# A hybrid encoder trunk: attention and recurrence issued in fixed rounds on TensorE

## The chip, the cores and the metric

The kernel runs on 1 core of one Trainium2 chip. Its time is device microseconds from launch to end, lower is better. A core has five engines with a queue each: PE (TensorE, matrix products and transposes), DVE (VectorE), ACT (ScalarE), POOL (GpSimd) and SP (SyncE, which issues most transfers). Products are written to PSUM, which has eight banks of 512 float32 columns for each of 128 partitions; DVE and ACT read them from there.

## What is computed

Two layers over 1024 tokens of width 1024. Layer 0 sends one input projection to two head groups: A, a recurrence with a delta rule (RWKV-7, 8 heads of 64), and B, sparse attention (8 heads of 64, one shared key and value, a mask that an index score chooses). The outputs are gated, joined and projected back. Layer 1 is gated linear attention. Each layer ends in a layer norm. The part that matters here, cut:

```python
# A, per token: state S of each head (64 x 64)
sa = einsum('bhvk,bhk->bhv', S, -kk_t)
S = S * w_t[:, :, None, :] + sa[..., None] * b_t[:, :, None, :] + v_t[..., None] * k_t[:, :, None, :]
y = einsum('bhvk,bhk->bhv', S, r_t)
# B, per block of 128 queries
s = einsum('bqhd,bqkd->bqhk', qb, k_sel) * (B_HEAD_DIM ** -0.5)
p = softmax(where(valid, s, -1e30))
o = einsum('bqhk,bqkd->bqhd', p, v_sel)
# both gated, joined, projected, then layer norm
y = concatenate([ya * silu(g_a), yb * silu(g_b)], -1) @ e_w_out
h = layer_norm(DN_ALPHA * h + y)
```

## The kernel before

The program is written in a tile framework: the author writes operations, and the framework allots buffers, adds semaphores and puts the instructions of each engine in an order by a simulated timeline. An engine then runs its queue in that order. `inorder` can pin an instruction to the order of the program text; with `PIN = 0` (line 35) it does nothing, so that the order on PE is the framework's own.

The change concerns one stage, from about 475 to 805 us of the profile. It holds three things.

**Attention.** For each of 8 tiles of 128 queries, `att_logits` forms for each head up to two banks of logits (L811, L812, into banks "s"); DVE adds the mask and takes the maximum (L813); ACT takes the exponential (L822), after every second head (`HG = 2`). `att_out` transposes the weights (L849, bank "st"), and the copies to SBUF (L851) go to DVE and ACT half and half (`EVD`). The products with the values (L833) collect in bank "po"; L864 multiplies by the gate and L865 stores the tile.

**Recurrence.** The 1024 tokens are 16 chunks of 64; two chunks are a unit, so there are 8 units. `products` (L978, bank "g", four bursts for a unit, each read by ACT at L980 and by DVE at L981 and L982) and `increments` (L987, bank "x") prepare a unit. `substitute` inverts its triangular blocks: POOL takes the diagonal blocks out (`mm`, L995, through the helper line L83), DVE sums them (`md`, L997), two transfers through DRAM bring them into another layout (L998, L1001), POOL runs 15 dependent steps (L1009, L1010), two more transfers bring the result back (L1013, L1015), and POOL spreads it (`TT`, L1017, again L83). `offdiag` completes the inverse in four steps on PE (L1035, L1044, L1054, L1063), the first after a transpose on DVE (`Tn`, L1030). `chain` then carries the state through the two chunks, three dependent steps each: Z (L1080), U (L1091 and L1096), Y (L1103), with copies on DVE and ACT between them (L1082 and L1083, L1097 and L1098, L1111 and L1113). Z and U of all heads lie in bank "zu", the outputs and states in bank "sy". `finish` normalises, gates and stores a unit's output.

**Output projection.** When attention has been issued in full, `open_pieces` frees its memory and loads the projection weights: 16 loads (L155), each split by ACT (L159) and POOL (L83). `piece` is one of 16 blocks of 128 tokens by 512 columns, 24 matmuls each (L764 to L766).

**Order.** `chain` calls `slot` six times for each unit. A slot asks the attention generator for some estimated microseconds (`att`, with the credits `ATT`), issues the preparation of the unit two ahead (`PREP`), and the off-diagonal steps of the next unit (`OFF`). In `PREP` the second half of the products ("q") and the whole of `substitute` ("s") come in slot 2; the loads for the second chunk stand directly before its products. The first two units are prepared before the chain starts. Buffers: `td`, `mm`, `md` and `BK` are single, `W` has 5, `RUV` 7.

Of the kernel before, what the change touches and what calls it, by code (L numbers as in the profile page):

```python
# [21 lines left out]
P = 128  # L22
SEQ = 1024
NT = 8
# [10 lines left out]
PIN = 0  # L35
# [7 lines left out]
FIN = 2  # L43
# [8 lines left out]
ATT, ATT1, ATT2, FC = (2.2, 1.2, 1, 10)  # L52
# [11 lines left out]
def trunk(ctx: ExitStack, tc: tile.TileContext, x, positions, e_w_in, a_mu, a_w0, a_w2, a_a0, a_a2,  # L64
# [10 lines left out]
    def cut(f, out, *ins):  # L75

        n = out.shape[1]
        each = 1
        for m in out.shape[2:]:
            each *= m  # L80
        w = max(1, PIECE // each)
        for a in range(0, n, w):
            f(out[:, a:min(n, a + w)], *(z[:, a:min(n, a + w)] for z in ins))  # L83
# [4 lines left out]
    def gmul(out, a, b):  # L88
        cut(G.tensor_mul, out, a, b)
# [671 lines left out]
    def out_piece(pt, yh, yl, wb):  # L761
        for k in range(NK):
            wh, wl = wb[k]
            PE.matmul(pt, yh[:, k, :], wh, start=(k == 0), stop=False)  # L764
            PE.matmul(pt, yh[:, k, :], wl, start=False, stop=False)  # L765
            PE.matmul(pt, yl[:, k, :], wh, start=False, stop=(k == NK - 1))  # L766
# [17 lines left out]
    open_psum("ps1", 0, s=2)  # L784
# [10 lines left out]
    def inorder(ins):  # L795
        if PIN:
            tc.keep_in_program_order(ins)

    def att_logits(i, w):

        n = P * (i + 1)
        qT = aw([P, 8, P], "qT", 2, F32R)
        nc.sync.dma_start(f32(qT), d_q[i])
        bias = cmask[:, 256 - n:] if i < 2 else bias_s[:, soff[i]:soff[i] + n]
        mx, m, rsum = aw([P, 8, 2], "mx", 2), aw([P, 8], "am", 2), aw([P, 8], "rsum", 2)
        ps = [aw([P, SEQ], "p", PB) for h in range(8)]
        w.extend((ps, rsum))
        for h in range(8):
            for z, (a, b) in enumerate(banks(n)):
                pt = ptile("s")[:, :b - a]  # L810
                inorder(PE.matmul(pt, qT[:, h, :], KH2[:, a:b], start=True, stop=False))  # L811
                inorder(PE.matmul(pt, qT[:, h, :], KL[:, a:b], start=False, stop=True))  # L812
                V.tensor_tensor_reduce(ps[h][:, a:b], pt, bias[:, a:b], 1.0, -3e38, op0=ALU.add, op1=ALU.max,  # L813
                                       accum_out=mx[:, h, z:z + 1])
            yield n / 1200
            if h % HG == HG - 1:
                hs = slice(h + 1 - HG, h + 1)
                if i >= 4:
                    V.tensor_max(mx[:, hs, 0], mx[:, hs, 0], mx[:, hs, 1])
                V.tensor_scalar(m[:, hs], mx[:, hs, 0], -0.125, None, op0=ALU.mult)  # L820
                for k in range(h + 1 - HG, h + 1):
                    A.activation(ps[k][:, :n], ps[k][:, :n], AF.Exp, scale=0.125, bias=m[:, k:k + 1],  # L822
                                 accum_out=rsum[:, k:k + 1])

    def att_out(i, w):
        ps, rsum = w
        po = ptile("po")

        def values(kt, pT):
            last = None  # L830
            for c in range(0, 512, PVN):
                for s in (1, 0):
                    last = after(last, PE.matmul(po[RS[s], c:c + PVN], v_tm[:, kt, :], pT[s][:, c:c + PVN],  # L833
                                                 start=(kt == 0 and c == 0), stop=(kt == i), skip_group_check=True))


        rb = aw([P, 8, CH], "rb")
        V.tensor_scalar(rsum, rsum, 2.0, None, op0=ALU.mult)
        V.reciprocal(rsum, rsum)
        A.copy(rb, rsum[:, :, None].to_broadcast([P, 8, CH]))  # L840
        g = aw([P, 4, P], "g")
        nc.sync.dma_start(g, d_gate[4:8, :, i * P:(i + 1) * P].rearrange("j p t -> p j t"))
        last = None
        for kt in range(i + 1):
            pT = []
            for s in range(2):
                pt = ptile("st")
                for j in range(4):
                    inorder(PE.transpose(pt[:, j * P:(j + 1) * P], ps[2 * j + s][:, kt * P:(kt + 1) * P], ident))  # L849
                pT.append(aw([P, 512], "pT", 4))  # L850
                (V.tensor_copy if (s + kt) % 4 in EVD else A.copy)(pT[s], pt)  # L851
                yield 0.45
                if s == 0 and last is not None:
                    values(kt - 1, last)
                    yield 1.0
            last = pT
        pt = ptile("st")
        for j in range(4):
            inorder(PE.transpose(pt[:, j * P:(j + 1) * P], rb[:, 2 * j:2 * j + 2, :].rearrange("p s d -> p (s d)"), ident))
        g2 = g.rearrange("p j t -> p (j t)")  # L860
        V.tensor_mul(g2, pt, g2)
        yield 0.45
        values(i, last)
        V.tensor_mul(g2, po, g2)  # L864
        nc.sync.dma_start(d_y[4:8, :, i * P:(i + 1) * P].rearrange("j p t -> p j t"), g)  # L865
        yield 1.0

    def attention():

        w = []  # L870
        yield from att_logits(0, w)
        for i in range(NT):
            w, o = [], att_out(i, w)
            m = att_logits(i + 1, w) if i + 1 < NT else iter(())
            r = 8 / (3 * i + 4)
            x = 0
            for c in o:
                yield c
                x += r
                while x >= 1:  # L880
                    x -= 1
                    c = next(m, None)
                    if c is not None:
                        yield c
            yield from m
# [64 lines left out]
    def load_unit(u):  # L950

        BK, BD = rt([P, 8, P], "BK"), rt([P, 8, P], "BD")
        nc.sync.dma_start(BK.rearrange("p (j c) t -> p j c t", c=2), d_bk[:, :, 2 * u:2 * u + 2, :])
        nc.sync.dma_start(BD.rearrange("p (j c) t -> p j c t", c=2), d_bd[:, :, 2 * u:2 * u + 2, :])
        U_[u] = dict(BK=BK, BD=BD, AT=[], W=[], MAB=rt([P, 8, CH], "MAB", 2))

    def load_chunk(u, cc):
        c = 2 * u + cc
        S = ATB[c % 6]
        vs = d_vt[c * CH:(c + 1) * CH].rearrange("t (j s d) -> t s j d", s=2, d=CH)  # L960
        for s in range(2):
            G.memset(S[RS[1 - s], :, s, 0:CH], 0.0)
            nc.sync.dma_start(S[RS[s], :, s, :], d_ar[RS[s], :, c, :])
            nc.sync.dma_start(ruv(c)[RS[1 - s], :, s, :], vs[:, s])
        U_[u]["AT"].append(S)

    def products(u, cc):

        U = U_[u]
        BK, AT = U["BK"], U["AT"][cc]  # L970
        W = rt([P, 4, 4, CH], "W", 5)
        U["W"].append(W)
        MABv = U["MAB"].rearrange("p (j c) t -> p j c t", c=2)
        for s in range(2):
            b_, k2_ = RS[s], RS[1 - s]
            pt = ptile("g")
            for j in range(4):
                inorder(PE.matmul(pt[:, j * P:(j + 1) * P], BK[:, j * 2 + cc, :], AT[:, j, s, :], start=True, stop=True))  # L978
# [276 lines left out]
    for _ in ag:  # L1255
        pass
# [265 lines left out]
```

## Time and profile before

| | us |
|---|---|
| median of 3 runs | 1338.23 (1331.89 to 1341.52) |
| the profiled execution, whole | 1340.62 |
| its span in the profile | 1338.9 |
| PE busy in the span | 1225.0 |
| DVE busy | 799.2 |
| ACT busy | 584.1 |
| POOL busy | 442.8 |

The span runs from the first to the last instruction; 1.7 us of the profiled execution lie outside. The mean granted TensorE clock is 0.952 of full speed. "Busy" of PE counts the time in which some matmul is in flight. A label such as L83 or L159 is a helper's line and holds instructions of many tiles. "Idle before" is the time that the engine stood still just ahead of an instruction, and the arrow names what ended the wait.

### The profile page before, as it was taken

What the parts mean: (1) busy time and instruction counts of PE and PEld (TensorE: products, weight loads), DVE (VectorE), ACT (ScalarE), POOL (GpSimd) and SP (SyncE); (2) the same over time, 40 slices, a digit from 0 to 9 for tenths busy, and PEclk for the clock granted to TensorE, in tenths of its full rate; (3) what the DMA queues carried; (4) which work ended last, traced back from release to release, by engine and by line L of the source; (5) the groups of instructions that cost most, each with busy time, mean ns of one, the idle gap of its engine ahead of it and who ended that gap; (6) DMA issues with size and microseconds to landing.
All of it is one profiled execution on the core that took longest, in us unless ns stands there. A gap on an engine that the chain in (4) does not pass through costs nothing.

```text
span 1338.9 us, 22002 instructions
## 1 busy us (share of the span) xinstructions
PE 1225.0 (91%) x8141; PEld 959.8 (72%) x8141; DVE 799.2 (60%) x1856; ACT 584.1 (44%) x1217; POOL 442.8 (33%) x749
## 2 busy tenths in 40 slices
PE   7998798999889968889899799999999999998997
PEld 6986585666666756667667578776678878887785
DVE  5246769999999546578677545870511124453666
ACT  5247767769732335546455351132830123332100
POOL 3233731453447432444444360143030331142000
PEclk9998799898899979999899789999999999999999
DMA  6102311442515478245433287562010220023221
GB/s 204 41 1 79 111 40 32 125 111 71 150 53 144 109 205 205 61 102 146 99 79 81 75 258 251 189 203 63 1 38 25 63 63 1 1 64 123 82 91 59
DMA packets 164780, 130.51 MB, mean 97 GB/s; under 512 B 61441, under 2 KB 138289, under 8 KB 164673
## 3 DMA queue, kind: packets, MB, share of 16 engines
q1 hardware_dynamic: 161872, 122.72, 31.9%
q10 hardware_dynamic: 2800, 6.39, 1.5%
q8 instruction: 64, 1.05, 0.3%
q14 instruction: 44, 0.35, 0.1%
HBM read 86.08 MB, written 42.99 MB: 96 GB/s over the span
## 4 chain that ended last, share of the span: by engine, by line
PE 39%; DVE 20%; DMA 15%; POOL 11%; issue 10%; ACT 4%; SPq 2%; DVEq 0%; POOLq 0%; ACTq 0%
DVE junk L677 7%; PE dn L174 4%; PE dn L176 4%; PE dn L175 4%; POOL itmp L1009 2%; POOL Xt L1010 2%; PE op L766 2%; PE op L764 2%; PE op L765 2%; PE gt L197 2%; PE gt L196 2%; PE gt L198 2%; POOL wlo L83 2%; DMA wraw<-in_e_w_in_dram 2%; DMA d_t<-Xt 1%
## 5 line engine op out<-in xcount | busy, mean ns | idle before, releaser
L83 POOL TENSOR_TENSOR wlo<-wraw,whi 128x256 fp32r<-128x256 f32 (+1 forms) x160 | 116.1, 755 | 260.0 <-ACT whi L159 202.2
L174 PE MATMUL dn<-xh,chi 128*128 128x512 f32 x336 | 138.1, 411 | 3.8 <-DVE sh L503 2.6
L176 PE MATMUL dn<-xh,clo 128*128 128x512 f32 x336 | 138.2, 411 | 0.0
L175 PE MATMUL dn<-xl,chi 128*128 128x512 f32 x336 | 137.3, 409 | 0.0
L159 ACT CAST whi<-wraw 128x512 fp32r<-128x512 f32 (+1 forms) x80 | 48.8, 613 | 133.2 <-PE dn L175 67.8
L174 PEld LDWEIGHTS dn<-xh,chi 128*128 128x128 f32 x336 | 66.4, 198 | 23.9 <-issue 5.2
L176 PEld LDWEIGHTS dn<-xh,clo 128*128 128x128 f32 x336 | 66.3, 197 | 20.4 <-issue 6.5
L175 PEld LDWEIGHTS dn<-xl,chi 128*128 128x128 f32 x336 | 66.2, 197 | 17.9 <-issue 4.2
L83 POOL TENSOR_TENSOR clo<-craw,chi 128x256 fp32r<-128x256 f32 x84 | 75.5, 927 | 1.0
L411 DVE SCALAR_TENSOR_TENSOR sc<-rl,wi_s,sc 128x384 f32<-128x384 f32 (+5 forms) x42 | 45.8, 1090 | 23.1 <-ACT rl L406 20.7
L184 POOL CAST chi<-craw 128x1024 fp32r<-128x1024 f32 x21 | 24.8, 1180 | 102.2 <-PE dn L175 84.2
L83 POOL TENSOR_TENSOR vg<-vg,sg 128x256 f32<-128x256 f32 x32 | 24.1, 775 | 99.4 <-DVE vg L1444 54.5
L822 ACT ACTIVATE p<-p,am 128x128 f32<-128x128 f32 (+7 forms) x64 | 49.1, 768 | 17.9 <-DVE am L820 17.6
L849 PE MATMUL st<-ident,p 128*128 128x128 f32 x288 | 50.8, 294 | 4.5 <-ACT pT L851 4.3
L764 PE MATMUL s<-whi,yh 128*128 128x512 f32 x128 | 51.5, 405 | 2.7 <-ACT yh L1184 1.6
L813 DVE CUSTOM_DVE_ANT_0 p<-s,bias_s 128x512 f32<-128x512 f32 (+1 forms) x80 | 45.7, 588 | 13.1 <-PE s L812 11.9
L677 DVE TENSOR_SCALAR_CACHE_REDUCE junk<-khi,Hc 128x384 bf16<-128x384 int16 (+1 forms) x64 | 51.9, 810 | 1.7
L677 DVE TENSOR_SCALAR_CACHE_REDUCE junk<-klo,Lc 128x384 bf16<-128x384 int16 (+1 forms) x64 | 51.8, 809 | 1.6
L978 PE MATMUL g<-AT,BK 128*128 128x128 f32 x256 | 39.5, 301 | 13.9 <-DMA AT<-d_ar 5.0
L196 PE MATMUL gt<-whi,hh 128*128 128x512 f32 x128 | 51.9, 406 | 0.0
L764 PE MATMUL op<-whi,yh 128*128 128x512 f32 x128 | 51.3, 402 | 0.0
L198 PE MATMUL gt<-whi,hl 128*128 128x512 f32 x128 | 51.2, 400 | 0.0
(471 smaller groups left out, 3368.8 us busy)
## 6 DMA issues: line engine op xcount, KB each, us to landing
wraw<-in_o_w_in_dram SPq DMA_DIRECT2D x48, 256.0 KB
craw<-in_e_w_in_dram SPq DMA_DIRECT2D x21, 512.0 KB
xt<-in_x_dram SPq DMA_DIRECT2D x8, 512.0 KB
d_q<-qiT SPq DMA_DIRECT2D x8, 512.0 KB
d_ar<-ar SPq DMA_DIRECT2D x8, 512.0 KB
d_gate<-sg SPq DMA_DIRECT2D x8, 512.0 KB
qT<-d_q SPq DMA_DIRECT2D x8, 512.0 KB
BK<-d_bk SPq DMA_DIRECT2D x8, 512.0 KB
```

The costliest lines, as they stand in the source:

```text
L83: f(out[:, a:min(n, a + w)], *(z[:, a:min(n, a + w)] for z in ins))
L159: A.copy(hi, raw)
L174: PE.matmul(pst, wh[:, cs], ah[:, k, sl], start=(k == 0), stop=False)
L175: PE.matmul(pst, wh[:, cs], al[:, k, sl], start=False, stop=False)
L176: PE.matmul(pst, wl[:, cs], ah[:, k, sl], start=False, stop=(k == NK - 1))
L196: PE.matmul(pst, ah[:, k, sl], wh, start=(k == 0), stop=False)
L198: PE.matmul(pst, al[:, k, sl], wh, start=False, stop=(k == NK - 1))
L411: E.scalar_tensor_tensor(acc[:, a:b], r, w, acc[:, a:b], op0=ALU.mult, op1=ALU.add)
L677: V.tensor_scalar(junk[:, :n], x, c[:, z:z + 1], None, op0=ALU.is_ge, op1=ALU.add, accum_out=cnt[:, z:z + 1])
L764: PE.matmul(pt, yh[:, k, :], wh, start=(k == 0), stop=False)
L822: A.activation(ps[k][:, :n], ps[k][:, :n], AF.Exp, scale=0.125, bias=m[:, k:k + 1], accum_out=rsum[:, k:k + 1])
L849: inorder(PE.transpose(pt[:, j * P:(j + 1) * P], ps[2 * j + s][:, kt * P:(kt + 1) * P], ident))
```

## The change

The stage is written out as fixed rounds. `chain` is taken apart into `step_z`, `step_u` and `step_y`, and each unit has six rounds, one step in each. A round issues in this order: the step; `wide`, the value products of the weights that were transposed in earlier rounds; one off-diagonal step if its place comes (`OFR = (3, 4, 5, 6)`: steps 0, 1, 2 of the next unit in rounds 3, 4, 5, the last in the following round 0); and `narrow`, some attention items (`PACE`, 4/3 to 2 a round; an item is one transposed group or one set of inverses, 80 in all) with their share of the next tile's logits, mixed with the preparation named in `OWN` for the unit two ahead. `PIN_ = 1`: every PE instruction of the stage is pinned to that order. Ahead of unit 0 stand twelve rounds (`PRE`) with two items each, that is 24 items, tiles 0 to 3.

Banks: transposes and logits share three banks "s" (`SB = 3`, `STB = "s"`); the two bursts of a chunk's products go to banks "g" and "x" (`PBK`); the chain has one bank for each head parity, "ca" and "cb", each with Z/U and outputs/states of four heads. `EVD = []`: all copies of transposed weights go to ACT. `HG = 1`: the exponential follows each head.

`substitute` is cut in three: `diagonal` ("!": `mm`, `md`, the two transfers) in round 1, the 15 steps and the transfers back ("x") in round 2, and `spread` ("t", the `TT`) in round 2 of the next unit; manual edges put `spread` behind the latest `mm` on POOL and `Tn` behind the latest `md` on DVE. Loads of the unit three ahead are issued in rounds 4 and 5. Attention ends with unit 5; the projection weights are loaded from unit 6 on, and up to five pinned pieces go into the rounds 1 to 5 of unit 7 (`FP = 1`). Behind the stage only bank names change.

The core of the diff:

```diff
-PB, HG, EVD = (14, 2, [1, 3])
+HG = 1
+EVD = []
-PREP = ('p', '0', 'qs', '1', '', '')
-OFF = [[], [], [0], [1, 2], [3], []]
+PACE = (4 / 3, 4 / 3, 5 / 3, 5 / 3, 5 / 3, 5 / 3, 2, 2)
+FP = 1
+SB = 3
+STB = "s"
+PIN_ = 1
+PBK = 'gx'
+OWN = ('ab', 'cd!', 'xt0', '1f', 'l', 'm')
+OFR = (3, 4, 5, 6)
+PRE = ('', 'ab', 'cd!x', '0', '1lm', '', 'AB', 'CD!TX', '2', '3LM', '', '')
+PO0 = 8
...
+    def wide():
+        while ready:
+            i, kt, pT = ready.pop(0)
+            po, g = OUT[i]["po"], OUT[i]["g"]
             for c in range(0, 512, PVN):
                 for s in (1, 0):
...
+                    inorder(PE.matmul(po[RS[s], c:c + PVN], v_tm[:, kt, :], pT[s][:, c:c + PVN],
+                                      start=(kt == 0 and c == 0), stop=(kt == i), skip_group_check=True))
...
+    def narrow(n, own=()):
+        ts = [todo.pop(0) for _ in range(min(n, len(todo)))]
+        lg = [z for t in ts for z in t[1]]
+        order, rest = [], list(own)
+        for k in range(max(len(rest), len(lg))):
+            order += [z for z in (lg[k:k + 1] + rest[k:k + 1])]
+        m = max(1, len(ts))
+        for k in range(m):
+            if k < len(ts):
+                f, *a = ts[k][0]
+                f(*a)
+            for f, *a in order[len(order) * k // m:len(order) * (k + 1) // m]:
+                f(*a)
...
+        pt = ptile(PBK[s])
...
+    def spread(u):
+        own_ = own[:, None].to_broadcast([P, 8, 4, HB])
         TT = rt([P, 8, CH], "TT", 3)
+        for ins in gmul(TT.rearrange("p v (b t) -> p v b t", t=HB), U_[u]["td"][:, :, None, :].to_broadcast([P, 8, 4, HB]), own_):
+            after(LAST["mm"], ins)
...
+    def step_z(u, cc):
+        bank = [ptile(("ca", "cb")[s]).rearrange("p (z j d) -> p z j d", z=2, d=CH) for s in range(2)]
...
     for u in range(NT):
-        chain(u, slot)
+        w = u + 2
+        for r in range(6):
+            (step_z, step_u, step_y)[r % 3](u, r // 3)
+            wide()
+            for z, q in enumerate(OFR):
+                v = u + 1 if q < 6 else u
+                if q % 6 == r and (q < 6 or u) and v < NT:
+                    offdiag(v, z)
+            names = OWN[r]
+            mine = [z for z in bursts(w, names) if z[1] < NT and (z[1] in U_ or z[0] in (load_unit, load_at))]
+            if "f" in names and u:
+                mine.append((finish, u - 1))
+                done = u
+            x += PACE[u]
+            n, x = int(x), x - int(x)
+            narrow(n, mine)
+            if not todo and not ready and ep is None:
+                open_pieces()
+            elif not todo and ep is not None and u == NT - 1 and r >= FP and pieces[0][0] < done:
+                piece(*pieces.pop(0), pin=True)
```

## Rows read from the trace of the kernel before

**Rows 1.** Stretches: length, busy (records) of five engines, clock, DMA share, GB/s

```profile
475.00:552.20 77.20, 62.35 (x572) 46.74 (x572) 49.17 (x177) 40.17 (x111) 28.39 (x103) 0.89 0.65 168
552.20:758.80 206.60, 183.09 (x3171) 145.62 (x3172) 143.98 (x423) 105.90 (x248) 90.15 (x257) 0.95 0.39 93
805.00:890.00 85.00, 83.55 (x389) 67.47 (x388) 61.56 (x144) 19.27 (x35) 16.27 (x22) 1.00 0.71 234
605.00:640.00 35.00, 34.15 (x634) 27.02 (x633) 31.78 (x98) 21.60 (x51) 16.67 (x48) 1.00 0.58 144
470.00:760.00 290.00, 250.73 (x3800) 196.45 (x3800) 194.62 (x604) 146.24 (x359) 118.80 (x360) 0.94 0.47 115
```

**Rows 2.** Timelines, PE and one of DVE: start, duration, operation, records, [idle, releaser]

```profile
479.83 0.45 PE L811 MATMUL s<-KH,qT 128*128 128x128 f32 x1 [5.71 <-DMA qT<-d_q]
556.31 0.71 DVE L1030 STREAM_TRANSPOSE Tn<-TT 128x512 f32<-128x512 f32 x1 [4.56 <-POOL TT L83]
557.80 1.76 PE L978 MATMUL g<-AT,BK 128*128 128x128 f32 x8 [3.23 <-DVE W L982]
599.21 2.04 PE L978 MATMUL g<-AT,BK 128*128 128x128 f32 x8 [5.00 <-DMA AT<-d_ar]
657.96 1.05 PE L1035 MATMUL x<-Tn,MAB 32*32 32x16 f32 x64 [3.93 <-DVE Tn L1030]
749.54 1.05 PE L1035 MATMUL x<-Tn,MAB 32*32 32x16 f32 x64 [3.11 <-DVE Tn L1030]
```

**Rows 3.** Timeline of POOL in the round trip of one substitution

```profile
659.11 1.57 POOL L83 TENSOR_TENSOR mm<-MAB,own 128x256 f32<-128x256 f32 x2
669.02 0.21 POOL L1009 TENSOR_TENSOR itmp<-Mt,Xt 128x15 f32<-128x15 f32 x1 [8.35 <-DMA Mt<-d_m]
680.36 0.22 POOL L1010 TENSOR_TENSOR Xt<-Xt,itmp 128x8 f32<-128x8 f32 x1
685.84 1.41 POOL L83 TENSOR_TENSOR TT<-td,own 128x256 f32<-128x256 f32 x2 [2.06 <-DMA td<-d_t]
691.90 1.42 POOL L83 TENSOR_TENSOR mm<-MAB,own 128x256 f32<-128x256 f32 x2 [1.41 <-ACT MAB L980]
```

**Rows 4.** Waits from 475 to 760 us: total us, times, longest

```profile
POOL itmp L1009 <- DMA Mt<-d_m: 48.4, 6, 13.8
ACT RUV L1098 <- DVE RUV L1097: 17.5, 4, 8.8
```

**Rows 5.** A slice of 5 us behind a wait, columns as in rows 1

```profile
655.00:660.00 5.00, 1.79 (x78) 1.69 (x80) 2.81 (x7) 0.63 (x2) 4.04 (x8) 0.71 0.76 200
```

**Rows 6.** Groups by line from 470 to 760 us: records | busy, mean ns | idle before

```profile
L851 DVE COPY pT<-st 128x512 f32<-128x512 f32 x36 | 24.6, 683 | 8.0 <-PE st L849 7.8
L820 DVE TENSOR_SCALAR am<-mx 128x2 f32<-128x2 f32 x32 | 6.0, 188 | 0.6
L851 ACT COPY pT<-st 128x512 f32<-128x512 f32 x36 | 21.1, 586 | 18.0 <-PE st L849 17.7
```

**Rows 7.** Groups by line on PE, the same stretch and columns

```profile
L1103 PE MATMUL sy<-RUV,W 128*64 128x64 f32 x448 | 20.4, 237 | 0.0
L1080 PE MATMUL zu<-RUV,AT 128*64 128x64 f32 x240 | 11.7, 227 | 1.3 <-DVE RUV L1111 0.9
L1035 PE MATMUL x<-Tn,MAB 32*32 32x16 f32 x512 | 7.3, 191 | 7.1 <-DVE Tn L1030 7.0
```

**Rows 8.** The end: timelines of PE, SP, POOL; L764 alone in a stretch

```profile
757.74 1.08 PE L833 MATMUL po<-pT,v_tm 128*64 128x256 f32 x8
763.36 1.78 SPq L155 DMA_DIRECT2D wraw<-in_e_w_out_dram  x4
776.10 10.67 POOL L83 TENSOR_TENSOR wlo<-wraw,whi 128x256 fp32r<-128x256 f32 x14 [2.70 <-DMA wraw<-in_e_w_out_dram]
789.28 1.04 PE L1103 MATMUL sy<-RUV,W 128*64 128x64 f32 x28 [0.53 <-ACT RUV L1098]
763.00:790.30 27.30, 7.24 (x17) 3.44 (x17) 0.75 0.78 242
```

More of the change, by code (lines that the diff above doesn't have):

```diff
@@ L804, in att_logits @@
         bias = cmask[:, 256 - n:] if i < 2 else bias_s[:, soff[i]:soff[i] + n]
[L805 to L830, printed above, removed]
+        for z, (a, b) in enumerate(banks(n)):
+            pt = ptile("s")[:, :b - a]
+            inorder(PE.matmul(pt, QT_[i][:, h, :], KH2[:, a:b], start=True, stop=False))
+            inorder(PE.matmul(pt, QT_[i][:, h, :], KL[:, a:b], start=False, stop=True))
+            V.tensor_tensor_reduce(ps[h][:, a:b], pt, bias[:, a:b], 1.0, -3e38, op0=ALU.add, op1=ALU.max,
+                                   accum_out=mx[:, h, z:z + 1])
@@ L832, in values @@
                 for s in (1, 0):
[L833 to L856, printed above, removed]
@@ new lines, in step_u @@
+    def step_u(u, cc):
+        bank, R, Zs, AT = CH_["bank"], CH_["R"], CH_["Zs"], CH_["AT"]
+        for j in range(4):
+            for s in range(2):
+                inorder(PE.matmul(bank[s][RS[1 - s], 1, j, :], AT[:, j, s, CH:], R[:, j, s, :], start=(j == 0),
+                                  stop=False, skip_group_check=True))
+        for j in range(4):
+            for s in range(2):
+                inorder(PE.matmul(bank[s][RS[s], 0, j, :], U_[u]["TT"][:, j * 2 + cc, :], Zs[:, j, s, :], start=True, stop=True))
+        CH_["R2"] = [V.tensor_copy(R[RS[0], :, 0, :], bank[0][RS[0], 0]), A.copy(R[RS[1], :, 1, :], bank[1][RS[1], 0])]
@@ new lines, in step_y @@
+    def step_y(u, cc):
+        U, c = U_[u], u * 2 + cc
+        bank, SP, R, W = CH_["bank"], CH_["SP"], CH_["R"], U["W"][cc]
+        if cc == 0:
+            U["Y"] = rt([P, 8, CH], "Y", 2)
+        Y = U["Y"]
+        for j in range(4):
+            for s in range(2):
+                for z in (1 - s, s):
+                    o = bank[s][RS[z], 1, j, :]
+                    inorder(PE.matmul(o, W[:, j, 2 * s + z, :], R[:, j, s, :], start=(z == s and j == 0), stop=True,
+                                      skip_group_check=True))
+        if c < 15:
+            Rn = ruv(c + 1)
+        for s in range(2):
+            if c < 15:
+                if c == 0:
+                    V.tensor_copy(Rn[RS[s], :, s, :], bank[s][RS[s], 1])
+                else:
+                    V.tensor_add(Rn[RS[s], :, s, :], bank[s][RS[s], 1], SP[RS[s]])
+            z = 1 - s
+            A.copy(Y[RS[1 - z], cc * 4:cc * 4 + 4, :], bank[z][RS[1 - z], 1])
+        if cc:
+            normed_heads(u, Y)
+            del U_[u]
+        del RUV[c]
@@ L1253, in trunk, with bursts @@
-    for u in range(NT):
-        chain(u, slot)
-    for _ in ag:
-        pass
+    traced = nc.cur_bb.bb.instructions
+    first = len(traced)
+    load_q(0)
+    load_unit(0)
+    load_at(0, 1)
+    load_q(1)
+    for h in range(8):
+        logits(0, h)
+    def bursts(u, names):
+        out = []
+        for z in names:
+            if z in "abcd":
+                z = "abcd".index(z)
+                out.append((products, u, z // 2, z % 2))
+            elif z in "01":
+                out.append((increments, u, int(z)))
+            elif z in "!xt":
+                out.append(({"!": diagonal, "x": substitute, "t": spread}[z], u - (z == "t")))
+            elif z == "l":
+                out.append((load_unit, u + 1))
+            elif z == "m":
+                out.append((load_at, u + 1, 1))
+        return out
@@ L1257, in trunk @@
+    wide()
+    for e in PINS:
+        last = None
+        for i in list(traced[first:]):
+            if str(i.engine).split(".")[-1] == e and i.opcode not in ("DMACopy",):
+                if last is not None:
+                    tc.add_manual_dep(i, last.name, mybir.DependencyInfo(
+                        mybir.DependencyClass.NoSync, mybir.DependencyReason.DATA), reason="in order")
+                last = i
     finish(NT - 1)
```

302 lines of the change are left out of this document (129 added, 173 removed).

## The prediction

> **What bounds the kernel now.** I read the busy time of the engines by stretches first, then PE's timeline with its waits, then the waits in total, then POOL's timeline behind the longest of them. The change touches only what stands between about 475 and 805 us. Behind it, from 805 to 890 us, PE is busy in 83.55 of 85 us at full clock [rows 1]: there PE is the bound, so a microsecond that the stage saves moves the end by one.
>
> In the stage the first step U of the chain stands at 552.2 us, and attention ends at 757.74 + 1.08 = 758.8 us [rows 8]. In these 206.6 us PE is busy in 183.1 and idle in 23.5; the mean granted clock is 0.95 [rows 1]. The clock has two levels, so a mean of 0.95 is 2 x 0.05 x 206.6 = 20.7 us at the lower one, which costs half of itself, 10.3 us. Four waits make 3.23 + 5.00 + 3.93 + 3.11 = 15.3 us of the idle time [rows 2], and the low clock stands behind them: 0.71 in the slice that follows the third [rows 5].
>
> Two of the four name `Tn`, DVE's transpose of `TT`; the first, at 557.80, ends on a product's copy on DVE, which had itself stood 4.56 us for `TT` of POOL until 556.31 [rows 2]. POOL's rows show why `TT` is late [rows 3]. `mm` ends at 660.7, the first step of the substitution starts at 669.0 (8.35 us of waiting for `Mt`), its last ends at 680.6, `TT` runs from 685.84 to 687.25 and the next `mm` follows at 691.90. From `mm` to `mm` 32.8 us pass, of which POOL spends most waiting for transfers, 48.4 us on `Mt` alone [rows 4]. The next unit's `mm` stands behind `TT` in POOL's queue, so the trip through DRAM is walked once a unit with nothing overlapped. The wait at 599.21 is a load issued just ahead of its use.
>
> Where no such wait falls, the stage is dense: from 605 to 640 us PE is busy 34.15 of 35 us and DVE 31.78, at full clock [rows 1]. So there is a second bound close behind, which limits what any new order can gain.
>
> **The start.** Products of a chunk come from two banks and both chunks stand in the first rounds, so the first substitution can begin earlier. But the twelve rounds do the work that the kernel before does ahead of 552.2 us (tiles 0 to 3, two units prepared), and in 475 to 552.2 us PE is busy 62.35 of 77.2 [rows 1]; of the 14.85 us idle 5.71 wait for the first `qT` [rows 2] and stay. Of the other 9.1 I take 4 as saved; none if the first `TT` still comes last, all 9 at best. **-4 us.**
>
> **Units 0 to 5.** Attention must still go beside them, 56 items in 36 rounds. I take the 206.6 us and correct them. The four long waits go, **-15.3**: `diagonal` stands one round ahead of the 15 steps and `spread` a unit later, so the 8.35 us and the trip back lie under other units' work; loads of `AT` and `BK` are issued in rounds 4 and 5, a round or more ahead. If SP holds those loads behind the store of `Xt`, which waits for POOL's 15 steps, the wait at 599.21 stays: then 10. With them goes the low clock, **-10.3**; half of it if short waits stay.
>
> Unit 6 is inside the 206.6 us before and behind attention afterwards. L1103 has 448 records for 14 chunks and 20.4 us, so 2.9 for a unit of two; L1080 has 11.7 us for 15 chunks, 1.6 a unit; the two groups of step U are of L1080's shape, 3.2; the off-diagonal step L1035 takes 7.3 / 8 = 0.9, and all four, taken alike, 3.6 [rows 7]. That is 11.3 us, which overlap other groups a little. **-10.**
>
> Against that stand new waits. PE is pinned now, so where it waits the rest of the round waits with it: behind a late step the value products, the off-diagonal step and all transposes and logits. DVE loses 36 copies, 24.6 us, and gains 32 more `am` operations of 0.19 us and some maxima, about 9 us; ACT gains 36 copies of 0.586 us, 21 us [rows 6]. From 470 to 760 us DVE then has 194.6 - 24.6 + 9 = 179 us of work and ACT 146.2 + 21 = 167 [rows 1]: both fit, but in units with logits DVE comes near PE. One bank for each head parity lets the two copies of a step run side by side, where ACT waited 17.5 us for DVE's `RUV` [rows 4]; that is latency inside a round, which other work hides, so I cost it at nothing (without that cover 0.4 us a step). `W` has five buffers and the sixth is asked for in round 1, before step Y frees one: the product's copy waits about a round and holds its bank, but the next use of that bank stands behind step Y on PE, so nothing comes of it. For small waits I take the rate of the dense stretch, 0.85 us idle in 35, plus as much again for the pinning: 178 us x 0.04 = **+7.** Below: 0. Above: a wait in every round for the copy of its last transposed group, 0.586 us with half of another such copy ahead of it in ACT's queue (an estimate from [rows 6]), 36 x 0.88 = 32 us.
>
> Sum: 206.6 - 15.3 - 10.3 - 10 + 7 = 178 us, so attention ends at 552.2 - 4 + 178 = 726 us instead of 758.8: 32.6 us earlier.
>
> **The end.** Before: the weights' first load is issued at 763.36, 4.6 us after attention; the chain ends at 790.3, and by then L764 has run 17 times, 8 of which make a piece: 2.1 pieces [rows 8]. A matmul of the following stretch costs 83.55 / 389 = 0.215 us [rows 1], a piece of 24 then 5.2, so 13.9 pieces are 72 us: attention end + 104. After: the load again 4.6 us behind attention; the eighth weight's lower half was ready 776.10 + 8 x 0.76 - 763.36 = 18.8 us after the first load [rows 8], so pieces can start at attention end + 23.4. Unit 6, 10 us of work, fits in that, so its latency and low clock cost nothing unless it exceeds 23 us. Then five pieces (26 us), unit 7's own 7 us, 1 for the clock, and eleven pieces (57): attention end + 114. **+10 us** (3 if unit 6 covers the loads, 16 if the pinned pieces hold the chain). Attention ends before unit 6 now, and 11 of the 32.6 us are paid back here.
>
> Against the profiled execution: 1340.6 - 32.6 + 10.4 = 1318.4. That execution lay 2.4 us above the median of the runs, so I predict **1316 us**.
>
> **Rivals.** *More room than PE's busy time shows.* Between 552.2 and 758.8 us weight loads are busy 145.6 us only [rows 1], so work may close up further: no small waits (-7), all of the start (-5), the other 8.2 us of idle (23.5 - 15.3): 1296. Against it: DVE's 31.78 of 35. The Trainium skill ("Trainium Kernel Development and Optimization", Performance Expectations) says that matmul busy time misjudges the headroom because matmuls are pipelined, and that weight-load busy time is the measure; by it 61 us would be free instead of 23.5. The trace has DVE full where PE is full, so I give it little. Chance 0.13.
>
> *The copies on ACT pace the rounds.* Each round waits 0.88 us as above: 32 in place of 7, +25 over my sum, 1341, no change. For it: all copies of weights stand in one queue, and the exponentials in the same. Against: value products come a step later than their transposes. Chance 0.24.
>
> *Slower: `spread` behind the 15 steps on POOL.* Both are issued in round 2, the steps first in the text; nothing orders them but the framework. If POOL takes the steps first, `TT` comes 8.3 + 11.6 + 1.4 us after `mm` [rows 3], and `Tn` 0.7 later [rows 2], 22 us in all; the pinned step that needs it stands two rounds of 178 / 36 = 4.9 us behind, so PE waits 12 us in each of six units: +72, 1388. It decides from 6 us a unit on. Against it: the steps must wait for `Mt` while `spread`'s data is a unit old, and the framework orders by when data is ready: it did put `mm` first at 659.11 while the 15 steps waited [rows 3]. Chance 0.13.
>
> **How the numbers follow.** My case, 1303 to 1328 by its terms, has 0.50. Less than about 1% (13 us) can't be told from no change, so faster is below 1325, slower above 1351. Faster: 0.43 of mine, 0.13 of the first rival, 0.02 of the second: 0.58. Slower: 0.12 of the third, 0.02 of the second: 0.14. Same: 0.28. The range is 1289 (best bounds: -9, 0, +3, the idle rest partly) to 1350 (every round waits, and the end costs some more); it leaves out the third rival and the edges of the others.
>
> **What would show it.** Right: `mm` to `mm` on POOL overlaps the trip, with no wait of PE on `Tn` above 1 us; clock 0.98 or more from the first U to the end of attention; attention ends near 726, at the end of unit 5, in rounds of about 5 us; five pieces in unit 7, and PE full behind it. Wrong: PE waits for `Tn`, or for `pT` in most rounds; DVE full through units 0 to 3 and rounds of 6 us; or unit 6 takes over 25 us and the gain is given back at the end.

## The result and the profile after

The changed kernel takes 1317.94 us (median of four runs, 1315.61 to 1322.56) where the kernel before, on the same chip, takes 1337.84: a ratio of 0.986, 95% interval 0.9815 to 0.9905. Run again beside the last experiments, the same kernel took 1317.07, ratio 0.9872 (0.9844 to 0.9900). Predicted were 1316 us and "faster", so the number holds. Most of the way to it does not, as the stretches show.

In the profiled execution (span 1313.9 us, time 1315.61) the stage begins at 473.3 us with the first logits; the first U stands at 548.8, attention ends at 719.2, the chain at 780.4, the last piece of the output projection at 850.1. Of the stretches between them, with the columns of [rows 1], and the whole stage in the last line:

```profile
473.30:548.80 75.50, 63.94 (x600) 50.78 (x602) 48.35 (x206) 48.45 (x129) 28.73 (x104) 0.88 0.63 161
548.80:719.20 170.40, 154.22 (x2904) 125.62 (x2898) 122.86 (x384) 111.74 (x253) 84.29 (x243) 0.98 0.42 103
719.20:755.00 35.80, 16.19 (x364) 13.73 (x360) 18.58 (x44) 17.62 (x38) 23.75 (x39) 0.62 0.68 197
755.00:780.40 25.40, 25.40 (x208) 20.39 (x206) 8.60 (x17) 6.03 (x14) 4.99 (x8) 1.00 0.54 160
780.40:850.10 69.70, 69.70 (x327) 57.95 (x326) 43.91 (x107) 14.87 (x28) 6.90 (x8) 1.00 0.66 213
473.30:850.10 376.80, 329.46 (x4385) 268.48 (x4386) 242.30 (x756) 198.72 (x459) 148.66 (x400) 0.93 0.54 148
```

The whole stage of the kernel before, from its first logits to the same last piece, was this line:

```profile
479.80:874.20 394.40, 353.04 (x4394) 278.45 (x4395) 264.96 (x776) 180.53 (x425) 147.58 (x399) 0.94 0.53 145
```

The stage became 17.6 us shorter (this last line ends at the start of the last matmul, 0.4 us before its end). PE's busy time fell by 353.04 - 329.46 = 23.6 us, with the same matmuls; its idle time did not fall, it rose from 41.4 to 47.3 us. The remaining 2.3 us of the medians' 19.9 are not the stage's by these two profiles: ahead of it no instruction changed its place, and behind it only bank names changed.

To part this I cut the stage into slices of some 2.5 us. A slice with granted clock c spends 2(1 - c) of its time at the lower level (1.2 instead of 2.4 GHz), and half of PE's busy time there is lost. What remains is "busy at full clock". The width is that of a matmul's weights, the second number of the shape in PE's rows (128*128, 128*64, 32*32): I counted, over the matmuls in the order of their start, how often it differs from the one ahead (widths up to 32 counted as one). The kernels from the third line on are those of the experiments below.

| kernel | stage, us | busy at full clock | lost to the low clock | idle | changes of width |
|---|---|---|---|---|---|
| before | 394.4 | 334.0 | 19.0 | 41.4 | 243 |
| after | 376.8 | 312.2 | 17.2 | 47.3 | 139 |
| one_ahead | 525.8 | 311.5 | 38.7 | 175.6 | 134 |
| free_order | 398.1 | 336.3 | 22.7 | 39.1 | 243 |
| banks_before | 410.3 | 318.8 | 21.6 | 69.9 | 139 |
| copies_shared | 375.4 | 312.2 | 16.8 | 46.5 | 139 |
| values_apart | 384.5 | 320.3 | 16.6 | 47.6 | 185 |
| early_start | 378.4 | 312.4 | 16.0 | 50.1 | 139 |
| pieces_sooner | 370.3 | 311.7 | 18.0 | 40.6 | 142 |
| pace_32 | 378.6 | 314.1 | 21.5 | 42.9 | 143 |
| after_again | 377.8 | 312.0 | 18.8 | 46.9 | 139 |
| sooner_shared | 373.7 | 312.0 | 20.6 | 41.1 | 142 |
| sooner_pace | 374.5 | 312.9 | 19.9 | 41.7 | 144 |

One line does not follow the count: banks_before has 139 changes and yet 318.8 us. PE stops there 70 times in the stage instead of 49, and the tail of the last matmul before a stop counts as busy (a matmul of 128*128 counts some 270 ns before a stop and 110 before its like), which makes some 3 of the 6.6 us; the rest is open. The kernels before and after stop equally often (52 and 49 times), so their difference is not of this kind.

The last column is visible in the timelines. PE of the kernel before (start, duration, operation, shapes, records), some 8 us at full clock:

```profile
617.11 0.34 PE L812 MATMUL s<-KL,qT 128*128 128x384 f32 x1
617.38 1.23 PE L1103 MATMUL sy<-RUV,W 128*64 128x64 f32 x32
618.54 1.16 PE L978 MATMUL g<-AT,BK 128*128 128x128 f32 x8
619.53 0.60 PE L849 MATMUL st<-ident,p 128*128 128x128 f32 x4
...
620.88 0.69 PE L1080 MATMUL zu<-RUV,AT 128*64 128x64 f32 x16
621.50 0.66 PE L1147 MATMUL x<-ident,Y 128*128 128x128 f32 x4
622.08 0.57 PE L1091 MATMUL sy<-RUV,AT 128*64 128x64 f32 x12
622.58 1.16 PE L978 MATMUL g<-AT,BK 128*128 128x128 f32 x8
623.67 0.34 PE L1091 MATMUL sy<-RUV,AT 128*64 128x64 f32 x4
623.93 0.66 PE L849 MATMUL st<-ident,p 128*128 128x128 f32 x4
624.52 1.08 PE L833 MATMUL po<-pT,v_tm 128*64 128x256 f32 x8
625.53 0.50 PE L811 MATMUL s<-KH,qT 128*128 128x512 f32 x1
```

From 617.38 to 625.53 the width changes ten times, and the first part of a step U (L1091) is torn in two. PE of the changed kernel over a similar time (left out are more of the same width as the line above):

```profile
606.31 1.05 PE L1005 MATMUL x<-AT,BK 128*128 128x128 f32 x8
607.29 0.27 PE L1131 MATMUL ca<-RUV,AT 128*64 128x64 f32 x1
...
607.81 0.22 PE L1135 MATMUL cb<-Zs,TT 128*64 128x64 f32 x1
...
608.28 1.04 PE L876 MATMUL po<-pT,v_tm 128*64 128x256 f32 x8
609.24 0.66 PE L853 MATMUL s<-ident,p 128*128 128x128 f32 x4
...
612.87 0.34 PE L1148 MATMUL ca<-RUV,W 128*64 128x64 f32 x4
...
613.85 1.03 PE L876 MATMUL po<-pT,v_tm 128*64 128x256 f32 x8
614.82 0.66 PE L853 MATMUL s<-ident,p 128*128 128x128 f32 x4
```

Four changes in as long: a round puts the chain's step and the value products (both 64 columns) side by side, then everything of 128.

### The profile page after: what moved, and what is told of

Read it like the earlier page. It is cut to its first block, busy times and chain, and to the rows that moved or that the text cites. A ratio compares the mean times of both kernels' runs of the same rounds, so it can differ in the third digit from the quotient of the medians.

```text
span 1313.9 us, 22069 instructions
## 1 busy us (share of the span) xinstructions
PE 1193.3 (91%) x8141; PEld 942.7 (72%) x8141; DVE 789.9 (60%) x1868; ACT 602.5 (46%) x1253; POOL 442.2 (34%) x749
## 4 chain that ended last, share of the span: by engine, by line
PE 47%; DVE 20%; issue 9%; DMA 8%; ACT 7%; POOL 6%; SPq 1%; DVEq 0%; POOLq 0%; ACTq 0%
DVE junk L686 7%; PE op L774 7%; PE s L774 7%; PE dn L183 3%; PE dn L185 3%; PE dn L184 3%; PE gt L207 2%; PE gt L205 2%; PE gt L206 2%; POOL wlo L92 2%; PE s L853 2%; DMA wraw<-in_e_w_in_dram 1%; PE po L876 1%; PE dn L1465 1%; DVE sc L420 1%
## 5 line engine op out<-in xcount | busy, mean ns | idle before, releaser
L184 PEld LDWEIGHTS dn<-xl,chi 128*128 128x128 f32 x336 | 65.3, 194 | 16.8 <-issue 3.5
L193 POOL CAST chi<-craw 128x1024 fp32r<-128x1024 f32 x21 | 22.7, 1080 | 97.0 <-PE dn L184 79.7
L853 PE MATMUL s<-ident,p 128*128 128x128 f32 x288 | 48.4, 293 | 4.1 <-ACT pT L855 3.2
L206 PE MATMUL gt<-wlo,hh 128*128 128x512 f32 x128 | 51.0, 399 | 0.0
```

The lines of the kernel that those rows point to most:

```text
L184: PE.matmul(pst, wh[:, cs], al[:, k, sl], start=False, stop=False)
L206: PE.matmul(pst, ah[:, k, sl], wl, start=False, stop=False)
L853: inorder(PE.transpose(pt[:, j * P:(j + 1) * P], OUT[i]["ps"][2 * j + s][:, kt * P:(kt + 1) * P], ident))
```

## Experiments: is it the trip, the order, the banks or the copies?

The theory at first was the prediction's: GpSimd's trip through DRAM, taken two units ahead, no longer holds TensorE. The rivals were the other parts of the change. Four kernels undo one part each.

**One unit ahead (`one_ahead`).**

```diff
-OWN = ('ab', 'cd!', 'xt0', '1f', 'l', 'm')
-OFR = (3, 4, 5, 6)
-PRE = ('', 'ab', 'cd!x', '0', '1lm', '', 'AB', 'CD!TX', '2', '3LM', '', '')
+OWN = ('abcd!', 'x', 't0', '1f', 'l', 'm')
+OFR = (4, 5, 6, 6)
+PRE = ('', 'ab', 'cd!x', '0', '1lm', '', '', 't', '', '', '', '')
-                out.append(({"!": diagonal, "x": substitute, "t": spread}[z], u - (z == "t")))
+                out.append(({"!": diagonal, "x": substitute, "t": spread}[z], u))
-        w = u + 2
+        w = u + 1
```

> The products, diagonal, substitution, spreading and increments of a pair are put back one unit ahead instead of two, in rounds 0 to 2 of the unit before, with the blocks off the diagonal in rounds 4, 5 and 0; order, banks, copies and pace stay as in the changed kernel. Theory (the gain comes from taking GpSimd's trip through DRAM out of TensorE's way): from the end of round 0 to round 4 there are about 20 us, the trip takes 26.7 us [mm to TT, before], so TensorE stands 3 to 7 us for Tn in each of six units and the clock falls there; first U to attention end 190 to 210 us instead of 170.4, whole 1333 to 1355. Rival (the fixed order, the banks or the copies brought the gain): the stretch stays within 5 us of 170.4 and the whole at 1313 to 1325.

Measured: 1468.28 us, ratio 1.099 (1.096 to 1.103). The mechanism is the theory's; its size, 15 us a unit, is far above the 3 to 7 that I gave. PE's waits in the stretch of the units (total us, times, longest):

```profile
PE x L1074 <- DVE Tn L1069: 89.1, 6, 16.5
```

One of the six, as PE and POOL show it, and last a seventh, behind attention:

```profile
598.14 1.41 POOL L92 TENSOR_TENSOR mm<-MAB,own 128x256 f32<-128x256 f32 x2 [10.32 <-ACT MAB L1007]
608.16 1.03 PE L876 MATMUL po<-pT,v_tm 128*64 128x256 f32 x8
624.81 1.05 PE L1074 MATMUL x<-Tn,MAB 32*32 32x16 f32 x64 [15.62 <-DVE Tn L1069]
622.52 1.40 POOL L92 TENSOR_TENSOR TT<-td,own 128x256 f32<-128x256 f32 x2 [2.04 <-DMA td<-d_t]
887.93 1.05 PE L1074 MATMUL x<-Tn,MAB 32*32 32x16 f32 x64 [42.77 <-DVE Tn L1069]
```

From `mm` to the end of `TT` 25.8 us pass, somewhat less than before the change (28.1 by [rows 3]); the rounds between hold some 10 us of work, and a fixed order cannot fetch more. The kernel before waited only 3 to 4 us for the same trip [rows 2]; the order that the framework had chosen holds other work there. In the seventh, POOL's 15 steps take 35 us instead of 11.6 [rows 3], since splits of the projection weights stand between them in its queue. Together the seven make 131.9 us, about the 128.3 us by which the stage's idle time exceeds the changed kernel's. Busy time at full clock stays at 311.5: the order saves as much as before, but it needs the two units ahead.

**Order left to the framework (`free_order`).**

```diff
-PIN_ = 1
+PIN_ = 0
```

> TensorE's instructions are no longer kept in program order; the framework orders them by its own estimate, as before the change. All else as in the changed kernel. Theory (two units ahead is what counts): no wait for Tn over 2 us between the first U and the end of attention, stretch 165 to 185 us, whole 1310 to 1330. Rival (the fixed order brought it): the stretch goes back to 195 to 210 us, whole 1335 to 1350.

Measured: 1360.66, ratio 1.018 (1.015 to 1.021). Neither came as stated: the whole lies 11 us above the rival's range, and the stretch, 145.4 us, below the theory's. There is no wait for `Tn` over 2 us, attention even ends at 694.7; but busy time at full clock is back at 336.3, with 243 changes of width, and the chain, left behind, ends so late (825) that the last pieces wait 24.0 us for their operand. Two units ahead without the order lose 1.8% against the kernel before.

**Banks as before (`banks_before`).** (The diff's core; the steps' operands follow.)

```diff
-SB = 3
-STB = "s"
-PBK = 'gx'
+SB = 2
+STB = "st"
+PBK = 'gg'
-        bank = [ptile(("ca", "cb")[s]).rearrange("p (z j d) -> p z j d", z=2, d=CH) for s in range(2)]
+        zu = ptile("zu").rearrange("p (z j d) -> p z j d", z=2, d=CH)
+        sy = ptile("sy").rearrange("p (s j d) -> p s j d", s=2, d=CH)
```

> Banks as before the change: both halves of the products in bank g, logits on two banks and transposes on one of their own, Z and U of both parities in one bank and outputs with next state in another. To build without a deadlock the W tiles have 6 buffers instead of 5 and the TT tiles 2 instead of 3. Theory (banks are not what counts, since neither pT nor a product waited over 1 us for a bank): stretch 168 to 178 us, whole 1315 to 1326. Rival (the banks brought a part): TensorE waits for pT and for evictions of g in most rounds, stretch over 180 us, whole over 1330.

Measured: 1353.66, ratio 1.014 (1.010 to 1.017): the rival. Idle time is 69.9 instead of 47.3 us, in many small waits; by the profile, step Z for its operand (first line), transposes for the copy that frees their one bank (second), products for ACT (third; PE, 470 to 900 us):

```profile
PE zu L1117 <- DVE RUV L1159: 10.3, 8, 5.5
PE st L853 <- ACT pT L855: 8.8, 12, 2.9
PE g L1005 <- ACT p L834: 5.1, 3, 2.2
```

The buffers of `W` and `TT` differ too in this kernel, so not all of its 33.5 us in the stage need be the banks'. What it shows is that I looked for the banks' worth in the changed kernel's waits, where they are absent because the banks are there.

**Copies shared (`copies_shared`).**

```diff
-EVD = []
+EVD = [1, 3]
```

> Half of the pT copies are VectorE's again, as before the change, the rest as in the changed kernel. Theory (neither engine sets the pace: ScalarE is busy 111.7 and VectorE 122.9 of 170.4 us): VectorE takes some 12 us more, the stretch changes by under 4 us, whole 1312 to 1324. Rival (the copies on ScalarE pace the rounds): the waits for pT (16.9 us in 26 times) go and the stretch shortens by 8 us or more, whole 1305 to 1310.

Measured: 1316.65, ratio 0.9856 (0.9824 to 0.9888), stage 375.4: no difference that can be told, as the theory says. (The 16.9 us quoted there are ScalarE's waits for TensorE, not the other way round.) The second rival of the prediction, copies that pace the rounds, is refuted.

## Experiments: why the same matmuls take less time

So the order makes TensorE's work itself shorter. The new theory: what costs is a change of width, and the fixed rounds have 104 fewer. The rival: neighbours don't matter, only the waits do.

**Value products behind the first transposes (`values_apart`).** The order stays fixed; only one group moves within the round.

```diff
             (step_z, step_u, step_y)[r % 3](u, r // 3)
-            wide()
+            late = len(ready)
...
                 f, *a = ts[k][0]
                 f(*a)
+            if k == 0:
+                wide(late)
```

> In the rounds of the units the value products of the round before (64 columns of weights) no longer stand right behind the chain's step (64 columns too) but behind the round's first transposes (128 columns). Same instructions, all else as in the changed kernel. Background, from the traces: with stretches at half clock counted at full clock, TensorE is busy 333.9 us of the stage before the change and 312.1 after it, though the instructions are the same; idle time and time lost to the low clock rise together from 60.4 to 64.7 us. Between neighbouring matmuls the width of the weights (128, 64 or 32 columns) changes 243 times before and 139 times after; a matmul ahead of a change takes some 100 to 200 ns more. New theory (the fixed rounds save TensorE time because matmuls of one width stand together): some 70 changes more, 0.1 to 0.17 us each, so full-clock busy time up by 7 to 12 us and the whole at 1324 to 1332. Rival (what was predicted: the gain is waits and clock, the neighbours don't matter): full-clock busy time within 2 us of 312 and the whole at 1313 to 1321.

Measured: 1323.51, ratio 0.9894 (0.9879 to 0.9909). The whole is just under the theory's range, and its interval overlaps that of the changed kernel, so by itself it would not decide. Busy time does: the edit makes 46 changes more, not 70, and at full clock it rises by 320.3 - 312.2 = 8.1 us, 0.18 us for each, where four profiles of the order with 139 changes agree within 0.4 us (after, after_again, copies_shared, early_start); idle and low clock stay. The place in PE's timeline:

```profile
612.89 0.23 PE L1138 MATMUL cb<-Zs,TT 128*64 128x64 f32 x1
...
613.05 0.66 PE L853 MATMUL s<-ident,p 128*128 128x128 f32 x4
613.64 1.08 PE L877 MATMUL po<-pT,v_tm 128*64 128x256 f32 x8
614.65 0.50 PE L824 MATMUL s<-KH,qT 128*128 128x512 f32 x1
```

**The change of width by itself (`widths`, run once).** The whole kernel is replaced by two loads and this, with weights of 128 columns in bank `a` and of 64 (then 32) columns in bank `b`:

```python
    for name, other, run in (("apart64", wide64, 16), ("mixed64", wide64, 1), ("apart32", wide32, 16), ("mixed32", wide32, 1)):
        a, b = bank(name + "a"), bank(name + "b")
        for _ in range(64 // run):
            for _ in range(run):
                wide128(a)
            for _ in range(run):
                other(b)
```

> Computes nothing of the reference (its output is zeros): TensorE alone runs 64 blocks of 8 matmuls with weights of 128 columns and 64 blocks of 8 with weights of 64 columns, once with the two kinds in turns of 16 blocks (8 turns, tiles apart64) and once block by block (128 turns, tiles mixed64); then the same with 32 columns (apart32, mixed32). Nothing is waited for but the loads at the start. Theory (a change of the width costs by itself, 0.176 us each as in values_apart): mixed64 takes some 21 us longer than apart64 for its 120 changes more, mixed32 some 15 to 25 us longer than apart32. Rival (not the width: what costs in the kernel is the waits that stand at such a change): mixed and apart within 3 us of each other.

Its four parts, in this order, with the columns length, PE, PEld, DVE, POOL, clock, DMA share, GB/s:

```profile
5.40:153.40 148.00, 147.96 (x2048) 147.27 (x2048) 0.17 (x1) 0.00 (x0) 1.00 0.01 2
153.40:319.60 166.20, 166.20 (x2052) 154.13 (x2048) 0.35 (x2) 0.00 (x0) 1.00 0.01 2
319.60:459.00 139.40, 131.04 (x2053) 130.00 (x2049) 0.35 (x2) 0.00 (x0) 0.95 0.01 2
459.00:604.00 145.00, 144.99 (x2053) 135.31 (x2048) 0.35 (x2) 0.00 (x0) 0.98 0.01 2
```

With 64 columns, 120 changes more cost 166.2 - 148.0 = 18.2 us, 0.15 us each; the 23 first matmuls of the part with few changes ran at half the pace (213 ns from start to start instead of 112; the clock's record begins only behind them, so the row reads 1.00), which hides some 2.6 us more, so 0.17. From start to start, a matmul of 128 columns takes 112 ns before its like and 205 before one of 64; one of 64 takes 30 before its like, on average of a pair, and 152 before one of 128. With 32 columns the part became only 5.6 us longer, not 15 to 25, because the part with few changes also stood idle for 8.4 us; busy time grows by 14.0 us, 0.12 each, and with the low clock taken out as above by 17.6, 0.15 each. The theory holds without any wait in play.

In the mixed parts the bank changes with the width, which would be another cause. The changed kernel's trace parts the two: there 776 matmuls of 64 columns that are followed by one of 64 in another bank take 34 ns from start to start on average, while the ten that are followed by another width take 151 to 192. In the kernel before, a matmul of 128*128 takes 110 ns before its like and 203 before one of 64 columns, as in this experiment. So it is the width.

104 changes at 0.15 to 0.18 us are 16 to 19 of the 21.8 us by which busy time at full clock fell. The other 3 to 6 are not accounted for.

The Trainium skill ("TensorEngine Tiling (Array Packing)", Key Properties) says that changing the tiling mode, not just the tile, drains TensorE; the page gives no price. These runs agree, with 0.15 to 0.18 us a change.

## Experiments: the start and the end

**Units 0 and 1 one round sooner (`early_start`).**

```diff
-PRE = ('', 'ab', 'cd!x', '0', '1lm', '', 'AB', 'CD!TX', '2', '3LM', '', '')
+PRE = ('ab', 'cd!x', '0', '1lm', '', 'AB', 'CD!TX', '2', '3LM', '', '', '')
```

> Products, diagonal, substitution and increments of units 0 and 1 each start one round of the warm-up sooner, the blocks off the diagonal of unit 0 stay where they are. Theory (the first unit's trip through DRAM is what TensorE stands for, 5.8 us at 525): the trip starts some 6 us sooner, that wait goes, first logits to first U 75.5 to 66..71 us, whole 1309 to 1315. Rival (the trip is paced by the loads of pair 1, which now also move ahead of it, or the products now wait for BK): the stretch stays at 74 to 78 us, whole 1315 to 1321.

Measured: 1319.28, ratio 0.9859 (0.984 to 0.9877); first logits to first U 74.5 us: the rival. The first products now stand 7.2 us for their load `BK` (PE's wait, below), and `TT` of unit 0 runs at 523.20 instead of 522.93. The loads set the start.

```profile
PE g L1005 <- DMA BK<-d_bk: 7.2, 1, 7.2
```

**Pieces from unit 6 on (`pieces_sooner`).**

```diff
-            elif not todo and ep is not None and u == NT - 1 and r >= FP and pieces[0][0] < done:
+            elif not todo and ep is not None and 6 * u + r >= 40 and pieces[0][0] < done:
```

> Pieces of the output projection may be taken from round 4 of unit 6 on instead of round 1 of unit 7. Theory (TensorE stands in unit 6 for want of other work: 19.6 us idle and 6.3 us lost to the low clock from the end of attention to the last piece): three more pieces of 5.1 us stand between the steps, the first some 8 us sooner, end of attention to last piece 120 to 127 us instead of 130.9, whole 1307 to 1314. Rival (the weights of the pieces land too late: the first request goes out 8.3 us after the end of attention, then eight blocks must be split): the first piece holds up the chain for the last wlo, 128 to 138 us, whole 1315 to 1325.

Measured: 1312.30, ratio 0.9811 (0.9794 to 0.9828). Seven pieces (168 matmuls) stand ahead of the chain's end instead of four (97), and end of attention to last piece is 127.4 us instead of 130.9, at the border of the theory's 127; the stage's idle time falls by 6.7 us. Of the 6.5 us that the stage is shorter, 2.5 lie ahead of the first U, where the edit changes nothing. The pieces start at 736.9 and wait some for `wlo`, the chain ends 13.6 us later in the execution, and it still pays.

**Some attention left for unit 6 (`pace_32`).** Units 2 to 5 take 9 items each instead of 10.

```diff
-PACE = (4 / 3, 4 / 3, 5 / 3, 5 / 3, 5 / 3, 5 / 3, 2, 2)
+PACE = (4 / 3, 4 / 3, 3 / 2, 3 / 2, 3 / 2, 3 / 2, 2, 2)
```

> Units 2 to 5 take 9 pieces of attention each instead of 10, unit 6 the last four. Theory (the light unit 6 is what costs): unit 6 loses 5 to 8 us of its idle time, but the weights of the output come some 8 us later against the chain, so one piece fewer stands in unit 7; whole 1312 to 1320. Rival (the room has to be idle somewhere, since the weights can only load when attention has ended): end of attention to last piece no shorter than 122 us while attention ends 8 to 12 us later, whole 1318 to 1328.

Measured: 1321.72, ratio 0.9892 (0.9869 to 0.9915). Attention ends 10.5 us later and the end is 9 us shorter (121.8): the idle time moved, as the rival has it.

**The best together.** `pieces_sooner` with the shared copies (`sooner_shared`), and that with two attention items moved from unit 5 to unit 6 (`sooner_pace`), beside the changed kernel as it is (`after_again`):

```diff
-EVD = []
+EVD = [1, 3]
...
-PACE = (4 / 3, 4 / 3, 5 / 3, 5 / 3, 5 / 3, 5 / 3, 2, 2)
+PACE = (4 / 3, 4 / 3, 5 / 3, 5 / 3, 5 / 3, 4 / 3, 2, 2)
```

> The changed kernel as it is, beside the next two on the same chip: 1313 to 1322, ratio to before 0.98 to 0.99 by either theory.

> pieces_sooner with half of the pT copies on VectorE (as in copies_shared). Theory (the two touch different stretches: the copies give 1.4 us in the units and the start, the sooner pieces 5.6): 1307 to 1313. Rival (both were scatter of single runs): 1313 to 1319.

> As sooner_shared, and unit 5 takes 8 pieces of attention instead of 10, so that the last two stand in round 0 of unit 6. Theory (unit 6 starts with 6.5 us of waiting for Tn of unit 7; two pieces more fill part of it): 1304 to 1312. Rival (the weights of the output then come later by as much): 1310 to 1318.

Measured: 1317.07, 1312.52 and 1312.88; ratios to before 0.9872 (0.9844 to 0.9900), 0.9838 (0.9819 to 0.9857), 0.9833 (0.9810 to 0.9857). The three kernels with sooner pieces lie some 4 to 6 us below the changed one, at the edge of the intervals. From end of attention to last piece they take 126.4 to 127.4 us, where the changed kernel takes 130.9 and 135.2 in its two profiles. The copies and the last shift of pace add nothing that can be told; 1312.88 is what the last rival has.

## Why the prediction was right in the number and where its steps failed

**The stretch of the units: -28.6 predicted, -36.2 measured.** The terms, one by one. Idle time was to lose 15.3 us and regain 7, so -8.3; it fell from 23.5 to 16.2, -7.3, and no wait of PE lasted over 1.71 us (that one for `Tn`, where I had said none above 1). Right. The low clock was to give back 10.3; by the slices only 8.9 were lost to it, since PE also stood still there, and the loss fell to 3.3, so 5.6, about the half that the prediction names for the case that short waits stay. The move of unit 6 was to take out 10; busy time at full clock fell by 174.2 - 150.9 = 23.3. So some 13 us came from a term that the sum doesn't have: PE's own work got shorter. (It is rather 17, since the first steps of unit 6 still ran beside attention and only 6.3 us of work stand between attention's end and unit 7.) In this stretch the changes of width fell from 193 to 96.

That is the step that failed: "so there is a second bound close behind, which limits what any new order can gain". I took 34.15 of 35 us busy [rows 1] for work, and work for a constant of the instructions. But busy time holds what a change of width costs, and the order decides how many there are. The first rival ("work may close up further") had the direction, and I set it to 0.13 because DVE was full beside it; DVE's busy time in the units fell as well, and did not bind. The Trainium skill's rule quoted there ("Trainium Kernel Development and Optimization", Performance Expectations) was right that busy time misjudges the room; but the weight loads, one of the two measures that it names, give no size either: over the stage they fell from 278.45 to 268.48 us, and PE's busy time by 23.6.

**POOL.** As told, `mm` and `TT` of the unit ahead stand together and the trip lies under other work. POOL in unit 5 and, last line, in unit 6:

```profile
700.80 1.42 POOL L92 TENSOR_TENSOR mm<-MAB,own 128x256 f32<-128x256 f32 x2 [4.45 <-ACT MAB L1007]
702.18 1.42 POOL L92 TENSOR_TENSOR TT<-td,own 128x256 f32<-128x256 f32 x2
726.72 1.40 POOL L92 TENSOR_TENSOR TT<-td,own 128x256 f32<-128x256 f32 x2 [4.68 <-DMA td<-d_t]
```

The third rival, `spread` behind the 15 steps, did not happen. POOL still waits 44.9 us for `Mt` from 473 to 760 us (48.4 in [rows 4]), but between the first unit and unit 6 no wait of PE over 1.71 us comes of it.

**The start: -4 predicted, +3.1 measured.** The bound "none if the first `TT` still comes last" was the case: PE stands 5.82 us for its transpose `Tn`, and early_start shows that the loads hold it.

```profile
525.22 1.05 PE L1074 MATMUL x<-Tn,MAB 32*32 32x16 f32 x64 [5.82 <-DVE Tn L1069]
```

**The end: +10.4 predicted, +15.5 measured.** The condition was there: the latency and low clock of unit 6 "cost nothing unless it exceeds 23 us". It took 32 us (714.5 to 746.8, from its first step Z to that of unit 7), 25 of them for its second half: with attention gone, each step is bare latency. PE's waits in it, and what stood in ACT's and SP's queues:

```profile
728.92 1.05 PE L1074 MATMUL x<-Tn,MAB 32*32 32x16 f32 x64 [6.70 <-DVE Tn L1069]
734.25 1.12 PE L1193 MATMUL x<-ident,Y 128*128 128x128 f32 x4 [4.28 <-ACT Gs L1076]
746.81 0.37 PE L1116 MATMUL ca<-RUV,AT 128*64 128x64 f32 x1 [3.98 <-ACT Y L1160]
...
730.71 1.22 ACT L168 CAST whi<-wraw 128x512 fp32r<-128x512 f32 x2 [8.08 <-DMA wraw<-in_e_w_out_dram]
733.93 0.27 ACT L1076 COPY Gs<-x 128x128 f32<-128x128 f32 x1
...
724.29 0.36 SPq L1047 DMA_DIRECT2D td<-d_t  x1
727.46 1.77 SPq L164 DMA_DIRECT2D wraw<-in_e_w_out_dram  x4
```

The copy `Gs` of 0.27 us stands behind casts of weights whose load has not landed; the weights' first load goes out 8.3 us behind attention, not 4.6 as in [rows 8], since in SP's queue the transfers `d_t` and `td` of unit 7 stand ahead of attention's last store, for which the load waits. The first piece stands 32.9 us behind attention, not 23.4, and four pieces go ahead of the chain's end instead of five. Both levels were set too low: attention end + 104 for the kernel before, which took 115.4, and + 114 for the changed one, which took 130.9. Most of that error stands on both sides and falls out of the difference.

**The sum.** Stage: -22.2 predicted (-4 - 28.6 + 10.4), -17.6 measured. Errors of +7, -7.6 and +5.1 us cancelled but for 4.6; and the profiled execution began the stage 6.5 us sooner, in instructions that stand in the same order before and after, of which the medians keep little. In the second profile of the same kernel the three parts take 75.1, 167.4 and 135.2 us, so the stage is known to about 1 us but its parts only to some 4. That the number was right with a term of 13 us or more missing is luck.

## What to carry to other kernels

Count how often TensorE changes the width of its weights before taking its busy time for its work: each change cost 0.15 to 0.18 us here, and the grouping of steps of one width was worth 16 to 19 us, more than the 12.9 us of idle time and low clock that went from the stretch of the units. A fixed order gives that grouping, but it can't walk around a wait; it paid only with the slow trip moved far enough ahead and with banks enough: with the order, the lead or the banks undone, the kernel was slower than before the change, by 1.8%, 9.9% and 1.4%. When a part is undone, look at idle time, low clock and busy time at full clock apart; the total hides opposite moves.

## What the runs showed of the hardware

A long run of short matmuls came to a stop. In `widths`, of 256 matmuls of 32*32 in a row, 223 started within 2 us, then PE stood for nothing that the profile shows:

```profile
348.41 2.04 PE L102 MATMUL apart32b<-M,W 32*32 32x16 f32 x223
352.60 0.66 PE L102 MATMUL apart32b<-M,W 32*32 32x16 f32 x33 [2.14 <-issue]
353.19 19.09 PE L90 MATMUL apart32a<-M,W 128*128 128x128 f32 x145
```

This happened in all four such runs of this part (8.4 us), and at each the granted clock fell for a while (0.68 over 352.0 to 362.5 us in this one); in blocks of eight (mixed32), from 464.5 us on, neither happened. Why PE stops there, and why the clock falls, is open.
